# Gate and up products of a gated MLP by seven block products per 128 features, the down product as a stage of its own

## The chip, the cores and the metric

The kernel runs on one core of a Trainium2 chip. The engines have short names in the profile: PE is the matrix engine (PEld its weight loads), DVE the vector engine, ACT the scalar engine, POOL the GpSimd engine, and SP issues most of the DMAs. The metric is the device time of one execution in microseconds (us), as the median of the runs.

## The reference, cut to what matters

One encoder layer over 512 tokens of 2048 features, all in float32: a mixer (retention and state-space heads), a gated MLP with 5632 features, and a gated per-layer input. The change is in the MLP and in the output projection that feeds it:

```python
hn = rmsnorm(h, norm_mix_w[i])
...
h = h + jnp.concatenate([ret, ssd], axis=-1) @ w_out[i]
hn = rmsnorm(h, norm_ffn_w[i])
h = h + conv_glu_ffn(hn, ffn_w_gate[i], ffn_w_up[i], ffn_conv_w[i], ffn_conv_b[i], ffn_w_down[i])
...
def conv_glu_ffn(h, w_gate, w_up, conv_w, conv_b, w_down):
    gate = depthwise_conv(h @ w_gate, conv_w, conv_b)
    return (jax.nn.gelu(gate, approximate=True) * (h @ w_up)) @ w_down
```

The convolution runs over tokens, with three taps. The norm of a token is a factor that the kernel applies after the products.

## The kernel before, in words

Activations lie feature-major: 128 features on the partitions, 512 tokens in the row. Each large product is float32 split exactly into two float32r parts, hi and lo, and takes three passes (`mm3`: hi by hi, hi by lo, lo by hi). A chunk is 128 output features over K = 2048, so 16 times 3 matmuls of 512 columns; each matmul loads its own 128 x 128 weights.

Weights come as a stream of units of 128 x 1024 (512 KB). SP fetches a unit into one of four `raw` tiles (`fetch`), ACT copies it to `whi` (L195), DVE subtracts to get `wlo` (L196), and there are three `whi`/`wlo` pairs. `next_unit` calls `split` two units ahead, so the split of unit i+2 waits until PE has left unit i-1, and has the time of two units.

The stages in order: mixer, output projection (16 chunks, DVE adds the residual at L874, ACT and POOL add up squares for the norm), MLP, per-layer input. After the projection every chunk of h is scaled and split into `xh`, `xl` (`operands`, L241, L242); the token norm (`token_norm`) goes through PE, DVE, POOL and PE again and ends in `Rb`, the norm on every partition. In the MLP, `ffn_order` lists 44 chunks "f" (gate, then up, two units each) and 11 groups "d" of the down product, each group after the four chunks that feed it. `ffn_chunk` takes the products out of PSUM with DVE (L887, L897), convolves (ACT L888, DVE L889 and L891), applies the gelu on ACT (L893), multiplies (L898) and splits the result into `ah`, `al` (L901, L902), which stay on chip. `down_group` has 8 units of 24 matmuls and adds to `h_t` in place (L917, 16 times a group). h stays on chip from the projection to the end.

Each engine runs its own instructions in order and waits on semaphores. The order is what a scheduler made of the program's order and of `tc.high_priority()`; what it made is shown below.

Of the kernel before, what the change touches and what calls it, by code (L numbers as in the profile page):

```python
# [17 lines left out]
F32 = mybir.dt.float32  # L18
# [8 lines left out]
P = 128  # L27
T = 512
# [25 lines left out]

XBC_ORDER = [8, 12, 10, 0, 1, 2, 3, 9, 11, 4, 5, 6, 7]
# [23 lines left out]
def layer(ctx: ExitStack, tc: tile.TileContext, xT, pT, pos, w_xbc, w_v, w_z, w_q, w_k, w_g,  # L79
# [42 lines left out]
    # ---------------------------------------------------------------- weight stream  # L122
# [19 lines left out]
    for n in range(KC):  # L142
        add_chunk(w_out, n)
    NG = FC // 4

    def ffn_order():
        order = [("f", c) for c in range(4)]
        for g in range(NG):
            if g + 1 < NG:
                order.append(("f", 4 * g + 4))  # L150
            order.append(("d", g))
            if g + 1 < NG:
                order += [("f", 4 * g + i) for i in (5, 6, 7)]
        return order

    for kind, i in ffn_order():
        if kind == "f":
            add_chunk(w_gate, i)
            add_chunk(w_up, i)
        else:  # L160
            for u in range(8):
                units.append(w_down[i, u])
# [12 lines left out]

    def fetch(i, pieces=1):
        if i < len(units) and i not in raws:
# [3 lines left out]
            raws[i] = r  # L181

    def split(i, pool=None, pieces=1):
        if i < len(units) and i not in splits:
            with tc.high_priority():
                fetch(i)
                r = raws[i]
# [10 lines left out]
                del raws[i]  # L198
                if not pool:
                    for j in range(i + 1, i + FETCH + 1):  # L200
                        fetch(j)
# [30 lines left out]
    cosR = const.tile([P, T], F32, name="cosR")  # L232
    sinR = const.tile([P, T], F32, name="sinR")
# [3 lines left out]
    # operand tiles: hi / lo of the moving activations, one per 128 features  # L237
# [18 lines left out]
    def gemm_chunk(xops):  # L256
        """128 output features x 512 tokens over K = 2048"""
# [5 lines left out]
    def ssq_mm(bank, sq, first, last):  # L263
        """bank[:, blk] += sum over the 128 partitions of sq[:, token]"""
# [11 lines left out]
    def diag_tokens(r, pool):  # L276
        """[128 tok, nb] column form -> hi and lo of its diagonal blocks"""
# [3 lines left out]
        dh = pool.tile([P, NB, P], F32R, name="bc_dh")[:, 0:nb]  # L281
        dl = pool.tile([P, NB, P], F32R, name="bc_dl")[:, 0:nb]
# [7 lines left out]
    def bcast_mm(dh, dl):  # L290
        """the column form on every partition: PSUM [128, 128 nb]"""
# [6 lines left out]
    def silu_of_half(dst, uh, th):  # L298
        """dst = silu(2 * uh)"""
# [24 lines left out]
    def token_norm(ss, pool, then=None):  # L324
        """two stages: sums and their rstd; Rb, the norm of each token on every partition"""
        box = []

        def one():
# [3 lines left out]
            box.append(diag_tokens(rcol, pool))  # L332
# [8 lines left out]
    # ================================================================ mixers  # L341
# [14 lines left out]
    # ---- start: x in, operands, token norms  # L356
    with tc.tile_pool(name="start", bufs=1) as st:
# [52 lines left out]
    # ---- SSD  # L410
    mix = ExitStack()
# [8 lines left out]
    # dt = softplus(.) and the decays; v's tile lends the room  # L420
# [706 lines left out]
```

## Time and profile before

| | |
|---|---|
| device time, median of 3 runs | 2573.64 us (2573.16 to 2577.39) |
| span of the profiled execution, first to last instruction | 2570.3 us |
| so outside the span, against the median | 3.3 us |
| PE busy | 2515.8 us (98%) |
| DVE, ACT, POOL busy | 1263.8, 804.3, 196.2 us |
| DMA moved | 257.33 MB, mean 100 GB/s |

The profile is of one execution. A matmul's length in it holds the pipeline's fill and drain, so the distance between two starts tells more than the length: successive matmuls overlap. The same holds, by a little, for instructions on DVE and ACT. The granted clock of PE (PEclk) is 1.00 when it has its full 2.4 GHz and 0.50 at 1.2 GHz.

### The profile page before, as it was taken

What the parts mean: (1) busy time and instruction counts of PE and PEld (TensorE: products, weight loads), DVE (VectorE), ACT (ScalarE), POOL (GpSimd) and SP (SyncE); (2) the same over time, 40 slices, a digit from 0 to 9 for tenths busy, and PEclk for the clock granted to TensorE, in tenths of its full rate; (3) what the DMA queues carried; (4) which work ended last, traced back from release to release, by engine and by line L of the source; (5) the groups of instructions that cost most, each with busy time, mean ns of one, the idle gap of its engine ahead of it and who ended that gap; (6) DMA issues with size and microseconds to landing.
All of it is one profiled execution on the core that took longest, in us unless ns stands there. A gap on an engine that the chain in (4) does not pass through costs nothing. (4 is left out here: it accounts for less than half of the span.)

```text
span 2570.3 us, 27344 instructions
## 1 busy us (share of the span) xinstructions
PE 2515.8 (98%) x11160; PEld 2068.8 (80%) x11160; DVE 1263.8 (49%) x1510; ACT 804.3 (31%) x1034; POOL 196.2 (8%) x136
## 2 busy tenths in 40 slices
PE   8988999999999999999999999999999999999997
PEld 6866678888888888888888888888888888887886
DVE  7887552665552254444344444444434444447344
ACT  4332343444332242222222222222222222225342
POOL 6023210000001100000000000000000000003111
PEclk9989999999999999999999999999999999999998
DMA  5333323232233333333333333333323333332332
GB/s 191 108 91 108 97 95 93 88 96 88 82 123 123 117 96 99 96 94 98 98 98 99 94 95 98 99 99 96 94 98 99 98 98 94 96 98 91 98 96 85
DMA packets 91326, 257.33 MB, mean 100 GB/s; under 512 B 8736, under 2 KB 29472, under 8 KB 91200
## 3 DMA queue, kind: packets, MB, share of 16 engines
q1 hardware_dynamic: 91056, 255.58, 32.0%
q8 instruction: 87, 1.43, 0.2%
q14 instruction: 39, 0.32, 0.0%
q10 hardware_dynamic: 144, 0.01, 0.0%
HBM read 251.29 MB, written 4.26 MB: 99 GB/s over the span
## 5 line engine op out<-in xcount | busy, mean ns | idle before, releaser
L211 PE MATMUL mm<-xh,whi 128*128 128x512 f32 (+1 forms) x2528 | 988.1, 391 | 5.8 <-ACT whi L195 5.0
L213 PE MATMUL mm<-xh,wlo 128*128 128x512 f32 (+1 forms) x2528 | 983.5, 389 | 4.0 <-DVE wlo L196 4.0
L212 PE MATMUL mm<-xl,whi 128*128 128x512 f32 (+1 forms) x2528 | 984.0, 389 | 2.0 <-DVE xl L242 2.0
L195 ACT CAST whi<-raw 128x1024 fp32r<-128x1024 f32 (+1 forms) x439 | 460.8, 1050 | 1282.7 <-PE mm L212 1194.1
L196 DVE TENSOR_TENSOR wlo<-raw,whi 128x1024 fp32r<-128x1024 f32 (+1 forms) x439 | 547.6, 1248 | 545.1 <-ACT whi L195 545.0
L211 PEld LDWEIGHTS mm<-xh,whi 128*128 128x128 f32 x2528 | 476.4, 188 | 105.3 <-ACT whi L195 5.5
L212 PEld LDWEIGHTS mm<-xl,whi 128*128 128x128 f32 x2528 | 476.1, 188 | 104.5 <-DVE xl L242 5.6
L213 PEld LDWEIGHTS mm<-xh,wlo 128*128 128x128 f32 x2528 | 476.2, 188 | 103.5 <-DVE wlo L196 5.6
L211 PE MATMUL mm<-ah,whi 128*128 128x512 f32 x704 | 274.1, 389 | 0.5 <-DVE h L917 0.5
L213 PE MATMUL mm<-ah,wlo 128*128 128x512 f32 x704 | 273.9, 389 | 0.0
L212 PE MATMUL mm<-al,whi 128*128 128x512 f32 x704 | 273.9, 389 | 0.0
L917 DVE TENSOR_TENSOR h<-h,mm 128x512 f32<-128x512 f32 x176 | 120.8, 687 | 207.6 <-PE mm L213 207.6
L322 POOL TENSOR_TENSOR ssq<-ssq,sq 128x512 f32<-128x512 f32 x52 | 80.9, 1556 | 1794.2 <-issue 1414.5
L211 PEld LDWEIGHTS mm<-ah,whi 128*128 128x128 f32 x704 | 132.1, 188 | 28.7 <-DVE h L917 0.7
L213 PEld LDWEIGHTS mm<-ah,wlo 128*128 128x128 f32 x704 | 132.1, 188 | 27.5
L212 PEld LDWEIGHTS mm<-al,whi 128*128 128x128 f32 x704 | 132.1, 188 | 27.4
L639 PE MATMUL mm<-whi,xh 128*128 128x512 f32 x256 | 106.4, 416 | 14.1 <-ACT v L649 9.2
L897 DVE TENSOR_TENSOR fup<-mm,Rb 128x512 f32<-128x512 f32 x44 | 30.4, 692 | 146.3 <-PE mm L213 146.3
L887 DVE TENSOR_TENSOR fpre<-mm,Rb 128x512 f32<-128x512 f32 x44 | 30.4, 692 | 144.2 <-PE mm L213 144.2
L640 PE MATMUL mm<-wlo,xh 128*128 128x512 f32 x256 | 100.9, 394 | 0.2 <-DVE wlo L196 0.2
L641 PE MATMUL mm<-whi,xl 128*128 128x512 f32 x256 | 100.8, 394 | 0.0
L639 PEld LDWEIGHTS mm<-whi,xh 128*128 128x128 f32 x256 | 48.9, 191 | 28.1 <-ACT v L649 10.0
(228 smaller groups left out, 1462.3 us busy)
## 6 DMA issues: line engine op xcount, KB each, us to landing
raw<-in_w_gate SPq DMA_DIRECT2D x88, 512.0 KB, 3.6
raw<-in_w_up SPq DMA_DIRECT2D x88, 512.0 KB, 3.6
raw<-in_w_down SPq DMA_DIRECT2D x88, 512.0 KB, 3.5
raw<-in_w_out SPq DMA_DIRECT2D x32, 512.0 KB, 3.6
raw<-in_w_ple SPq DMA_DIRECT2D x32, 512.0 KB, 3.6
raw<-in_w_xbc SPq DMA_DIRECT2D x25, 512.0 KB, 3.7
bc<-rows_d SPq DMA_DIRECT2D x16, 512.0 KB, 5.9
raw<-in_w_v SPq DMA_DIRECT2D x16, 512.0 KB, 3.5
```

Source lines behind the costliest of these rows:

```text
L195: S.copy(hi[:, sl], r[:, sl])
L196: V.tensor_tensor(lo[:, sl], r[:, sl], hi[:, sl].bitcast(F32), op=ALU.subtract)
L211: TE.matmul(out, lh, rh, start=start, stop=False)
L212: TE.matmul(out, lh, rl, start=False, stop=False)
L213: TE.matmul(out, ll, rh, start=False, stop=stop)
L322: G.tensor_tensor(self.acc, self.acc, sq, op=ALU.add)
L639: TE.matmul(banks[b], xh[:, sl], wh, start=(k == 0), stop=False)
L640: TE.matmul(banks[b], xh[:, sl], wl, start=False, stop=False)
L641: TE.matmul(banks[b], xl[:, sl], wh, start=False, stop=(k == KC - 1))
L887: V.tensor_tensor(pre, gb, Rb, op=ALU.mult)
L897: V.tensor_tensor(up, ub, Rb, op=ALU.mult)
L917: V.tensor_tensor(h_t[n], h_t[n], bank, op=ALU.add)
```

## The change

For each chunk of 128 features the weights are taken as four blocks of 128 x 1024: gate and up, each for the first and the second half of K. The activations are taken as four blocks too: two halves of K, each for the first and the second 256 tokens. Gate and up for both halves of the tokens then are a 2 x 2 block product, and it is made from seven products instead of eight, each with K = 1024 and 256 columns (`prod`: 8 times 3 matmuls). Three of the seven weight forms are sums (`weight_form`: four adds of 128 x 1024 on DVE a chunk, three of them in place), and each form is split to hi and lo as a unit was. The seven activation forms (`singles`, `sums`) are made once, from h scaled by the norm's weights, for 8 pairs of chunks (chunk j and j + 8, so the projection's order is changed to give them in pairs); for three pairs (EARLY) during the projection, for five after it. All are kept as hi and lo in `E`.

h goes to DRAM (`h_d`) and the 44 results of `ffn_chunk` too (`acts_d`), by DMAs that POOL issues. The down product runs after all 44 chunks, in six groups of K (five of two weight rows, one of one); the activations of a group are read back through a `fup` tile by POOL's DMAs and split by ACT and DVE, those of the next group during the current one. The matmuls of the down product are as many and as large as before; it adds to h 6 times 16 times instead of 11 times 16.

```diff
+DOWN = [(0, 1), (2, 3), (4, 5), (6, 7), (8, 9), (10,)]
...
+    for c in range(FC):
+        for k in FORMS:
+            units.append((c, k))
+    for ds in DOWN:
+        for u in range(8):
+            for d in ds:
+                units.append(w_down[d, u])
...
+        if k == 2:
+            V.tensor_tensor(w11, w11, w12, op=ALU.add)
+            gu_sum[c] = f6 = gu_pool[1].tile([P, 1024], F32, name="wsum", bufs=1)
+            V.tensor_tensor(f6, w11, w22, op=ALU.add)
+            return f6
+        if k == 3:
+            return w11
+        if k == 4:
+            V.tensor_tensor(w12, w12, w22, op=ALU.add)
+            return w12
+        if k == 5:
+            return w22
+        V.tensor_tensor(w21, gu_sum.pop(c), w21, op=ALU.add)
+        return w21
...
+    SLOT = (0, 1, 4, 3, 5, 6, 2)
...
+    def form_split(j, a, n, src):
+        hi, lo = (e[:, a:a + n] for e in E[j])
+        S.copy(hi, src)
+        V.tensor_tensor(lo, src, hi.bitcast(F32), op=ALU.subtract)
...
+    def singles(j):
+        form_split(j, 0, 1, xw[j][:, 0:1])
+        form_split(j, 1, 2, xw[j][:, 2:4])
...
+        if which == 0:
+            t = late_p.tile([P, 2, HT], F32, name="es", bufs=2)
+            V.tensor_tensor(t[:, 0], x21, x22, op=ALU.subtract)
+            V.tensor_tensor(t[:, 1], t[:, 0], x11, op=ALU.subtract)
+            form_split(j, 3, 2, t)
+        else:
+            V.tensor_tensor(x21, x11, x21, op=ALU.subtract)
+            V.tensor_tensor(x12, x12, x22, op=ALU.subtract)
+            V.tensor_tensor(x12, x12, x21, op=ALU.subtract)
+            form_split(j, 5, 2, xw[j][:, 1:3])
...
+        ss.add(hc)
+        nc.gpsimd.dma_start(h_d[n], hc)
...
+    for j in range(EARLY, KP):
+        singles(j)
+    for j in range(EARLY, KP):
+        sums(j, 0)
+    for j in range(EARLY, KP):
+        sums(j, 1)
+    norm_stages = token_norm(ss, late_p, tag="es")
...
+        hi, lo = (w.rearrange("p (k n) -> p k n", n=P) for w in next_unit())
+        for j in range(KP):
+            eh, el = (e[:, slot] for e in E[j])
+            mm3(out, hi[:, j], lo[:, j], eh, el, start and j == 0, stop and j == KP - 1, True)
+        tick()
...
+        R, PQ = mm_bank(), mm_bank()
+        r, p, q = R[:, 0:HT], PQ[:, 0:HT], PQ[:, HT:T]
+        prod(r, SLOT[0], True, True)
+        if c == 0:
+            norm_stages[0]()
+        prod(p, SLOT[1], True, True)
+        if c == 0:
+            norm_stages[1]()
...
+            S.copy(ab[:, 0:HT], r)
+        prod(r, SLOT[2], False, True)
...
+            S.activation(ab[:, HT:T], r, AF.Copy, scale=-1.0)
+        prod(q, SLOT[3], True, True)
...
+            S.copy(cc, q)
+        prod(r, SLOT[4], False, True)
...
+            V.tensor_tensor(up[:, HT:T], cc, r, op=ALU.subtract)
+        prod(q, SLOT[5], False, True)
...
+            V.tensor_tensor(s[:, :, 0:HT], PQ.rearrange("p (n t) -> p n t", n=2),
+                            ab.rearrange("p (n t) -> p n t", n=2), op=ALU.add)
+        V.tensor_tensor(up, up, Rb, op=ALU.mult)
+        prod(r, SLOT[6], False, True)
...
+        V.tensor_tensor(acc, up, acc, op=ALU.mult)
+        nc.gpsimd.dma_start(acts_d[c], acc)
...
+        a = main.tile([P, T], F32, name="fup", bufs=3)
+        nc.gpsimd.dma_start(a, acts_d[c])
+        hi = pool.tile([P, T], F32R, name=f"ah{c % 8}")
+        lo = pool.tile([P, T], F32R, name=f"al{c % 8}")
+        S.copy(hi, a)
+        V.tensor_tensor(lo, a, hi.bitcast(F32), op=ALU.subtract)
...
+    for c in chunks(0):
+        load_act(c, sides[0].p)
+    for n in range(KC):
+        nc.gpsimd.dma_start(h_t[n], h_d[n])
```

Where the instructions stand. DVE in a chunk of the middle of the MLP, before (L196 is the split of a weight unit, L887 and L897 take the products out of PSUM):

```order
L887 TENSOR_TENSOR fpre_10369<-mm_10308,Rb_74 128x512
L196 TENSOR_TENSOR wlo_10378<-raw_10245,whi_10377 128x1024
L889 SCALAR_TENSOR_TENSOR facc_10370<-fpre_10369,vec_69,facc_10370 128x511
L891 SCALAR_TENSOR_TENSOR facc_10370<-fpre_10369,vec_69,facc_10370 128x511
L196 TENSOR_TENSOR wlo_10408<-raw_10275,whi_10407 128x1024
L897 TENSOR_TENSOR fup_10437<-mm_10376,Rb_74 128x512
L898 TENSOR_TENSOR fup_10437<-fup_10437,facc_10370 128x512
L196 TENSOR_TENSOR wlo_10445<-raw_10313,whi_10444 128x1024
L902 TENSOR_TENSOR al_10441<-fup_10437,ah_10440 128x512
```

The same in the changed kernel, from the subtraction that follows product 4 (counted from 0) to the split of form 3 of the next chunk (`wlo` from `rawB` or `wsum` is the split of a weight form, L217, L219, L224, L228 are the weight sums):

```order
L1037 TENSOR_TENSOR s_11290<-cc_11289,mm_11227 128x256
L247 TENSOR_TENSOR wlo_11384<-rawB_11127,whi_11383 128x1024
L217 TENSOR_TENSOR rawB_11127<-rawB_11127,rawB_11190 128x1024
L1040 TENSOR_TENSOR s_11290<-mm_11228,ab_11288 128x2x256
L224 TENSOR_TENSOR rawB_11190<-rawB_11190,rawB_11192 128x1024
L219 TENSOR_TENSOR wsum_11459<-rawB_11127,rawB_11192 128x1024
L247 TENSOR_TENSOR wlo_11416<-rawB_11158,whi_11415 128x1024
L1042 TENSOR_TENSOR s_11290<-s_11290,Rb_80 128x512
L228 TENSOR_TENSOR rawB_11158<-wsum_11459,rawB_11158 128x1024
L247 TENSOR_TENSOR wlo_11462<-wsum_11459,whi_11461 128x1024
L247 TENSOR_TENSOR wlo_11490<-rawB_11127,whi_11489 128x1024
L1047 TENSOR_TENSOR s_11290<-s_11290,Rb_80 128x512
```

Before, one or two weight splits stand between two instructions that read PSUM; now all four weight sums and the splits of forms 0 to 3 follow L1037, with one reader of PSUM among them (L1040).

DVE at the start of the MLP, before (`xl` is the lo part of the last activations, L273 to L287 make the token norm's diagonal blocks):

```order
L242 SCALAR_TENSOR_TENSOR xl13_6469<-h_5344,vec_69,xh13_6468 128x512
L242 SCALAR_TENSOR_TENSOR xl14_6473<-h_5344,vec_69,xh14_6472 128x512
L242 SCALAR_TENSOR_TENSOR xl15_6477<-h_5344,vec_69,xh15_6476 128x512
L196 TENSOR_TENSOR wlo_6512<-raw_6319,whi_6511 128x1024
L273 TENSOR_SCALAR rstd_t_6531<-mx_6526 128x4
L284 CAST bc_rh_6534<-rcol_77 128x4
L285 TENSOR_TENSOR bc_dh_6536<-cst_70,bc_rh_6534 128x512
L286 TENSOR_TENSOR bc_rl_6535<-rcol_77,bc_rh_6534 128x4
L287 TENSOR_TENSOR bc_dl_6537<-cst_70,bc_rl_6535 128x512
L196 TENSOR_TENSOR wlo_6570<-raw_6356,whi_6569 128x1024
```

In the changed kernel, the end of that work (L932 is the lo part of an activation form, L951 to L953 are the sums of the last two, L338 and L340 the same diagonal blocks; the waits are in brackets):

```order
L247 TENSOR_TENSOR wlo_6743<-raw_6333,whi_6742 128x1024 [waits PE_49,Activation_49]
L932 TENSOR_TENSOR El5_6537<-xw5_6177,Eh5_6536 128x512 [waits Activation_49]
L952 TENSOR_TENSOR xw6_6318<-xw6_6318 128x256
L951 TENSOR_TENSOR xw7_6459<-xw7_6459 128x256
L953 TENSOR_TENSOR xw6_6318<-xw6_6318 128x256 [waits DVE_49]
L952 TENSOR_TENSOR xw7_6459<-xw7_6459 128x256
L338 TENSOR_TENSOR es_6655<-cst_76,bc_rh_6653 128x512
L932 TENSOR_TENSOR El6_6539<-xw6_6318,Eh6_6538 128x512 [waits Activation_49]
L953 TENSOR_TENSOR xw7_6459<-xw7_6459 128x256 [waits DVE_49]
L340 TENSOR_TENSOR es_6656<-cst_76,bc_rl_6654 128x512
L932 TENSOR_TENSOR El7_6541<-xw7_6459,Eh7_6540 128x512 [waits Activation_49]
L247 TENSOR_TENSOR wlo_6773<-raw_6329,whi_6772 128x1024 [waits PE_49,Activation_49]
```

The diagonal blocks of the norm, which came right after the last activation, now come behind nearly all of the late activation forms.

POOL at the end of the MLP, before (L322 adds squares, L274 is the power of the norm; no DMA is on this queue):

```order
L322 TENSOR_TENSOR ssq_15254<-ssq_15254,sq_15480 128x512
L322 TENSOR_TENSOR ssq_15254<-ssq_15254,sq_15503 128x512
L322 TENSOR_TENSOR ssq_15254<-ssq_15254,sq_15520 128x512
L274 TENSOR_TENSOR rcol_77<-rstd_t_15692,mhalf_73 128x4
L322 TENSOR_TENSOR ssq_15727<-ssq_15727,sq_15796 128x512
```

In the changed kernel, from its first instruction for the down stage (L1070 reads an activation, L1091 a chunk of h, L1055 writes an activation):

```order
L1070 DMA fup_16730<-acts_d_5346 128x512 [waits DMASW3_49,PE_49,Activation_49]
L1070 DMA fup_16736<-acts_d_5346 128x512 [waits DMASW4_49]
L1070 DMA fup_16742<-acts_d_5346 128x512 [waits DMASW5_49]
L1091 DMA h_16726<-h_d_5345 128x512 [waits DMASW6_49]
L1091 DMA h_16726<-h_d_5345 128x512 [waits DMASW7_49]
L1091 DMA h_16726<-h_d_5345 128x512 [waits DMASW0_49]
L1070 DMA fup_16748<-acts_d_5346 128x512 [waits DMASW3_49,DMASW1_49,DVE_49]
L1070 DMA fup_16754<-acts_d_5346 128x512 [waits DMASW4_49,DMASW2_49,DVE_49]
L1091 DMA h_16726<-h_d_5345 128x512
L1070 DMA fup_16760<-acts_d_5346 128x512 [waits DMASW5_49,DVE_49]
L1055 DMA acts_d_5346<-acc_16711 128x512 [waits DVE_49]
L1091 DMA h_16726<-h_d_5345 128x512 [waits DMASW6_49]
```

POOL now issues the loads of the first activations one by one, with loads of h and a store between them, and those from the fourth on wait for DVE to free a `fup` tile.

## Rows read from the trace of the kernel before

**Rows 1.** The page's part 1: busy time, share of the span, instructions of each engine.

```profile
PE 2515.8 (98%) x11160; PEld 2068.8 (80%) x11160; DVE 1263.8 (49%) x1510; ACT 804.3 (31%) x1034; POOL 196.2 (8%) x136
```

**Rows 2.** Stretches, from the MLP's first matmul to the down product's last.

```profile
913.08:2350.40 1437.32, 1436.82 (x6341) 1189.18 (x6340) 638.78 (x725) 381.54 (x425) 20.02 (x13) 1.00 0.31 96
```

**Rows 3.** The timeline of PE in the last chunk, 256 columns: start, length (us).

```profile
2539.39 0.28 PE L211 MATMUL mm<-xh,whi 128*128 128x256 f32 x1
2539.50 0.28 PE L212 MATMUL mm<-xl,whi 128*128 128x256 f32 x1
...
2548.74 0.50 PE L267 MATMUL mx<-ones,ssq 128*128 128x1 f32 x4
```

**Rows 4.** The timeline of weight loads (PEld) in the same stretch.

```profile
2539.39 0.19 PEld L212 LDWEIGHTS mm<-xl,whi 128*128 128x128 f32 x1
2539.50 0.19 PEld L213 LDWEIGHTS mm<-xh,wlo 128*128 128x128 f32 x1
```

**Rows 5.** Groups by form: count | busy us, mean ns of one | idle before.

```profile
L196 DVE TENSOR_TENSOR wlo<-raw,whi 128x1024 fp32r<-128x1024 f32 x437 | 546.2, 1251 | 544.2 <-ACT whi L195 544.1
L195 ACT CAST whi<-raw 128x1024 fp32r<-128x1024 f32 x437 | 459.5, 1052 | 1281.6 <-PE mm L212 1194.1 <-PE mm L641 55.4 <-issue 26.7
...
L322 POOL TENSOR_TENSOR ssq<-ssq,sq 128x512 f32<-128x512 f32 x52 | 80.9, 1556 | 1794.2 <-issue 1414.5 <-ACT sq L320 379.2
L888 ACT ACTIVATE facc<-fpre,vec 128x512 f32<-128x512 f32 x44 | 35.6, 810 | 1.4 <-DVE fpre L887 1.4
...
L891 DVE SCALAR_TENSOR_TENSOR facc<-fpre,vec,facc 128x511 f32<-128x511 f32 x44 | 33.0, 751 | 1.5
L887 DVE TENSOR_TENSOR fpre<-mm,Rb 128x512 f32<-128x512 f32 x44 | 30.4, 692 | 144.2 <-PE mm L213 144.2
...
L569 DVE TENSOR_TENSOR bc<-bc,A 128x1024 f32<-128x1024 f32 x8 | 12.3, 1535 | 17.7 <-POOL bc L566 17.7
...
L1023 DVE TENSOR_TENSOR h<-h,mx 128x256 f32<-128x256 f32 x12 | 4.4, 413 | 0.4 <-ACT facc L1014 0.4
L274 POOL TENSOR_TENSOR rcol<-rstd_t,mhalf 128x4 f32<-128x4 f32 x3 | 3.1, 1020 | 16.6 <-DVE rstd_t L273 16.6
```

**Rows 6.** The timeline of DVE in MLP chunks: start, length (us), idle before.

```profile
1207.17 0.69 DVE L887 TENSOR_TENSOR fpre<-mm,Rb 128x512 f32<-128x512 f32 x1 [3.35 <-PE mm L213]
1208.03 1.23 DVE L196 TENSOR_TENSOR wlo<-raw,whi 128x1024 fp32r<-128x1024 f32 x1 [0.17 <-ACT whi L195]
...
1218.05 0.69 DVE L897 TENSOR_TENSOR fup<-mm,Rb 128x512 f32<-128x512 f32 x1 [3.35 <-PE mm L213]
1218.77 0.69 DVE L898 TENSOR_TENSOR fup<-fup,facc 128x512 f32<-128x512 f32 x1
1219.38 1.22 DVE L196 TENSOR_TENSOR wlo<-raw,whi 128x1024 fp32r<-128x1024 f32 x1
1220.52 0.68 DVE L902 TENSOR_TENSOR al<-fup,ah 128x512 fp32r<-128x512 f32 x1
```

**Rows 7.** The timeline of ACT in the same chunk.

```profile
1206.94 1.05 ACT L195 CAST whi<-raw 128x1024 fp32r<-128x1024 f32 x1 [4.38 <-PE mm L212]
```

**Rows 8.** The timeline of PE there, the last two matmuls of a weight unit.

```profile
1206.51 0.39 PE L212 MATMUL mm<-xl,whi 128*128 128x512 f32 x1
1206.74 0.39 PE L213 MATMUL mm<-xh,wlo 128*128 128x512 f32 x1
```

**Rows 9.** Stretches of 2 us around PE's longest wait.

```profile
252.00:254.00 2.00, 0.00 (x0) 0.00 (x0) 0.04 (x1) 0.00 (x0) 0.00 (x0) 1.00 0.80 228
256.00:258.00 2.00, 0.01 (x1) 0.01 (x1) 0.10 (x1) 1.33 (x4) 1.87 (x2) 0.50 0.61 218
262.00:264.00 2.00, 0.80 (x4) 0.37 (x3) 1.81 (x2) 2.00 (x4) 0.00 (x0) 1.00 0.00 0
```

**Rows 10.** DMA issues by line: count, KB each, us to landing.

```profile
raw<-in_w_gate SPq DMA_DIRECT2D x88, 512.0 KB, 3.6
...
bc<-rows_d SPq DMA_DIRECT2D x16, 512.0 KB, 5.9
...
fup<-in_xT SPq DMA_DIRECT2D x16, 256.0 KB, 2.6
```

More of the change, by code (lines that the diff above doesn't have):

```diff
@@ L53 @@
 N_VEC = _n
+FORMS = range(7)
+KP = KC // 2
+EARLY = 3
+DOWN = [(0, 1), (2, 3), (4, 5), (6, 7), (8, 9), (10,)]
 XBC_ORDER = [8, 12, 10, 0, 1, 2, 3, 9, 11, 4, 5, 6, 7]
@@ L141, in layer @@
         add_chunk(w_g, h)
-    for n in range(KC):
+    OUT_ORDER = [n for j in range(KP) for n in (j, j + KP)]
+    for n in OUT_ORDER:
         add_chunk(w_out, n)
[L144 to L162, printed above, removed]
+    for c in range(FC):
[5 more added lines that the diff above has]
+                units.append(w_down[d, u])
     for n in range(KC):
@@ L197, in split @@
                 splits[i] = (hi, lo)
-                del raws[i]
                 if not pool:
-                    for j in range(i + 1, i + FETCH + 1):
+                    ahead = FETCH
+                    if i + FETCH < len(units) and isinstance(units[i + FETCH], tuple):
+                        ahead = 2 * FETCH
+                    for j in range(i + 1, i + ahead + 1):
                         fetch(j)
@@ new lines, in layer, with prod @@
+    ox.close()
+    opx.close()
+    g1 = ExitStack()
+    fb_p = g1.enter_context(tc.tile_pool(name="fb", bufs=1, reuse_waits="tile"))
+    gu_pool[1] = fb_p
+    for j in range(EARLY, KP):
+        form_tiles(j, fb_p)
+    for j in range(EARLY, KP):
+        singles(j)
+    for j in range(EARLY, KP):
+        sums(j, 0)
+    for j in range(EARLY, KP):
+        sums(j, 1)
+    norm_stages = token_norm(ss, late_p, tag="es")
+    m1 = None
+    def prod(out, slot, start, stop):
+        hi, lo = (w.rearrange("p (k n) -> p k n", n=P) for w in next_unit())
[3 more added lines that the diff above has]
+        tick()
@@ L865, in layer @@
+    for c in range(FC):
+        ffn_chunk(c)
+    g1.close()
+    fa.close()
     main = ctx.enter_context(tc.tile_pool(name="main", bufs=1, reuse_waits="tile"))
@@ new lines, in layer, with open_group, chunks, down_group @@
+    sides = {}
+    def open_group(g):
+        sides[g] = e = ExitStack()
+        e.p = e.enter_context(tc.tile_pool(name=f"acts{g}", bufs=1, side="left" if g % 2 else "right",
+                                           reuse_waits="tile"))
+    def chunks(g):
+        return [4 * d + k for d in DOWN[g] for k in range(4)]
+    open_group(0)
+    for c in chunks(0):
+        load_act(c, sides[0].p)
+    for n in range(KC):
+        nc.gpsimd.dma_start(h_t[n], h_d[n])
+    def down_group(g, ss):
+        last = g + 1 == len(DOWN)
+        if not last:
+            open_group(g + 1)
+            ahead = chunks(g + 1)
+        for u in range(8):
+            banks = [mm_bank(), mm_bank()]
+            for i, d in enumerate(DOWN[g]):
+                hi, lo = (w.rearrange("p (k n) -> p k n", n=2 * P) for w in next_unit())
+                for nn, bank in enumerate(banks):
+                    sl = slice(nn * P, (nn + 1) * P)
+                    for k in range(4):
+                        ah, al = acts[4 * d + k]
+                        mm3(bank, hi[:, k, sl], lo[:, k, sl], ah, al, i == 0 and k == 0,
+                            i + 1 == len(DOWN[g]) and k == 3)
+            for nn, bank in enumerate(banks):
+                n = 2 * u + nn
+                with tc.high_priority():
+                    V.tensor_tensor(h_t[n], h_t[n], bank, op=ALU.add)
+                if ss:
+                    ss.add(h_t[n])
+            if not last and u < len(ahead):
+                load_act(ahead[u], sides[g + 1].p)
+            tick()
+        if last:
+            sides[g].close()
+        else:
+            sides[g].close()
```

205 lines of the change are left out of this document (115 added, 90 removed).

## The prediction

> **What bounds the kernel now.** I read the page's busy times first. PE is busy 98% of a span of 2570.3 us, DVE 49%, ACT 31% [rows 1]: PE is the bound if it is dense and not merely overlapped with waits. So the stretch that the change rebuilds comes next, from the MLP's first matmul to the last of the down product: 1437.32 us, of which PE is busy 1436.82, at a granted clock of 1.00, DVE 639, ACT 382 [rows 2]. Its work is 44 x 2 x 48 = 4224 matmuls for gate and up and 11 x 8 x 24 = 2112 for down, 6336 of 512 columns: 1437.3 / 6336 = 0.2268 us each (a dozen small matmuls of the norm are in it). PE starts a matmul every 0.227 us there and waits for nobody; only fewer or shorter matmuls, or new waits, can change it.
>
> The new matmuls have 256 columns, each with its own weight load. The last chunk of the kernel is computed in two halves of the tokens, so the trace holds that form: 78 starts from 2539.39 to 2548.74 [rows 3], 0.1199 us each. That is 53% of 0.2268, not 50%; seven products instead of eight therefore give 7/8 x 2 x 0.53 = 0.925 of the time, not 0.875.
>
> **Gate and up.** Removed: 4224 x 0.2268 = 958.0 us. Added: 44 x 7 x 24 = 7392 matmuls x 0.1199 = 886.3 us. That is -71.7 us if PE stays dense. A product takes 24 x 0.1199 = 2.88 us, a chunk 20.1 us.
>
> Does DVE keep up? It is in order, and the spacing of its instructions counts, not their length: a split of 1024 follows its predecessor's start by 0.61 and is followed after 1.14 us (1218.77, 1219.38, 1220.52); an instruction that needs its predecessor's result waits for its end and 0.04 more (1218.05 to 1218.77) [rows 6]. The weight sums have no row; two-input instructions of 1024 lie between 1.25 us (the split, 437 of them) and 1.54 us (L569) [rows 5]. I take the split, which has the same size and two SBUF inputs as they have. A chunk is then 11 x 1.14 (7 splits, 4 sums) + 4 x 0.61 + 2 x 0.75 + 0.41 = 16.9 us of 20.1 [rows 5, 6]. ACT has 7 x 1.05 and six smaller ones of at most 0.81, below 12.3 us [rows 5].
>
> The tight place is the chain shown by the order, from the end of product 4 to the split of form 2 of the next chunk. PE's release reaches ACT 0.04 us after the last read of `whi` ends, and DVE 0.04 after ACT ends (1206.51 + 0.39 to 1206.94; 1207.99 to 1208.03) [rows 6 to 8]; a 256-column matmul is 0.28 long, so ACT begins 0.08 after product 5 has begun. Then 1.05 + 0.04 for `whi`, split 1.29, sum 1.14, PSUM 0.61, sums 2 x 1.14, split 1.14, `up` 0.61, sum 1.14, split 1.29: 10.7 us in all. PE needs that `wlo` at the third matmul of product 2: 4 x 2.88 + 0.24 = 11.8 us later. The slack is 1.1 us, so I cost the steady chunk at nothing. The waits on PSUM have more: each accumulator is read while a 2.88 us product runs on the other bank. Behind a late DVE the splits of all later forms queue, and PE waits for them.
>
> The weights are as many bytes, 2 MB per 20.1 us, fetched 8 forms ahead (23 us) against 3.6 us to landing [rows 10]: hidden.
>
> **Start of the MLP.** Before, this is seamless. Now no activation form of five pairs exists when the projection ends, and DVE makes them. Counting from the last projection matmul: DVE adds the residual until 0.9, ACT squares until 1.6, POOL issues a store of h and adds (1.56 us) until about 3.5, PE sums, DVE reads at 4.1, POOL's power takes 1.02 [rows 5], and DVE, which is in order, goes on at 5.4. From there to the second diagonal block and the splits around it stand 7 x 1.14 (2 sums, 5 splits) + 17 x 0.61 (15 lo parts, 2 diagonals) + 24 x 0.34 (256 wide: 0.41 long, less the 0.07 that a successor overlaps) = 26.5 us, with 2 us of in-place waits and one wait for PE: 34 us. Products 0 and 1, which follow the lo parts pair by pair, end near 14.5, product 3 near 25. The norm's broadcast is next on PE and waits for a diagonal block near 31.7. ACT then copies `Rb` and the first product (1.0), and four products remain: 31.7 + 0.5 + 1.0 + 11.5 = 44.7. PE's clock: after 8 us without matmuls the granted clock stood at 0.50 and was 1.00 again six us later [rows 9]; PE idles 7 us here, which I put at +2. So the first chunk takes 47 us instead of 20: +27. Bounds: 16 if POOL and DVE overlap better and the clock holds; 40 if every DVE instruction takes its full length (34 becomes 39) and all five last products run at half speed.
>
> **Down.** The matmuls are the same: 2112 x 0.2268 = 479.0. The first activations must come back from DRAM after the last MLP matmul, since their tiles lie where the activation forms were. POOL-issued DMAs have no row; 256 KB from SP lands in 2.6 us, the slowest kind of row takes 5.9 [rows 10]. I take 3 with a microsecond of POOL per issue (its shortest instruction in rows 5 is 1.02): first at 3.4, `ah0` and `al0` at 4.8, the fourth activation at 11, the eighth at 18, because three `fup` tiles cycle and loads of h stand in POOL's queue between them. PE does what it can meanwhile (11 of 21.8 us of the first two weight rows): +8. Bounds: 4, with issue at nothing and 2.6; 18, with 5.9 in each of three rounds. DVE's 80 fewer adds of h (11 x 16 to 6 x 16) were hidden and gain nothing. Later groups load during the group before: 8 loads in 87 us. The hand-over to the per-layer input keeps its form: 0, give or take 2; likewise the projection, where DVE gains 4.5 us of work per pair in a 21.8 us window.
>
> [...]
>
> **Sum.** 886.3 + 27 + 479.0 + 8 = 1400.3 against 1437.3: -37 us. The span becomes 2533.3; the median of the runs lies 3.3 us above the span of the profiled execution, so 2536.6.
>
> **Rivals.**
> 1. DVE becomes the bound. If its 1024-wide instructions, with sums in place, take the 1.54 us of L569, the seven in the chain cost 7 x 0.4 = 2.8 us more, less 1.1 of slack: 1.7 x 44 = +75, so 2611, slower. It decides against the change from 1.1 + 37/44 = 1.94 us, that is from 1.42 us per instruction. For it: DVE's work in a chunk nearly doubles and has only 3 us to spare. Against: 437 splits average 1.25.
> 2. The hand-overs eat the gain: 72 us instead of 35, with both upper bounds and 14 more in the first chunks of each stage. 2574, no change.
> 3. Weight loads become the bound. PEld is 80% busy already [rows 1] and a load lasts 0.19 us [rows 4]; one after the other, 7392 x 0.19 would be 1404 instead of 886: about 3055, slower. The Trainium skill, "Perfetto Trace Analysis", section "Identifying the Most-Contended Engine", judges PE by just this share and not by matmul time, which would make the change a loss. Against: at 256 columns loads start 0.11 to 0.12 us apart and overlap [rows 4], 78 times in a row [rows 3].
> 4. The hand-overs cost half, since the scheduler's order lets PE go on earlier: 35 becomes 18, so 2519.
>
> **How the numbers follow.** My forecast has 0.77, its own range 2521 to 2558 (both lower bounds; 40 for the start, 18 for down). Rival 1 has 0.08, rival 2 0.06, rival 3 0.02, rival 4 0.07. For 8 in 10 I take 2516 to 2564. The runs can tell a change of 0.2% (5 us): faster is the forecast, rival 4 and a part of rival 2, 0.87; same 0.04; slower 0.09.
>
> **What would show it.** Matmul starts 0.12 us apart through the MLP, PE over 99% busy in a middle chunk of 20.1 us, and 43 of them. If chunks take longer and PE waits for `wlo`, rival 1 is at work, and the lengths of the sums say why; if it waits with weight loads back to back, rival 3. In the first chunk PE should wait for the lo parts and then long for the diagonal blocks, some 27 us in all; at the start of down for `ah` and `al`, some 8. The prediction is wrong if the 256-column pitch does not hold at full rate for 886 us, or if either hand-over costs more than twice its term.

## The result, and the profile after

The changed kernel takes 2544.27 us (median of 4 runs, 2541.68 to 2545.18) against 2573.4 of the kernel before on the same chip: a ratio of 0.9887, 95% interval 0.9873 to 0.9901, so 29 us faster. Forecast were 2536.6, between 2516 and 2564. The profiled execution has a span of 2541.9 us, 28.4 less than before. By the terms of the sum:

| term | predicted, us | profile, us |
|---|---|---|
| gate and up, 44 steady chunks | 886.3 | 883.0 (44 x 20.067) |
| first chunk, over a steady one | +27 | +27.5 (47.52 - 20.07) |
| hand-over to down | +8 | +7.2 (5.2 to the first matmul, 2.0 in the first group) |
| the matmuls of down | 479.0 | 486.6 |
| per-layer input | 0 | +4.1 |
| ahead of the MLP | 0 | +0.6 |
| all, against before | -37 | -28.4 |

The terms that were hard to size came out right by size. The two that were carried over unchanged (down and the per-layer input) are the ones that failed. Part 1 of the page, the answer to [rows 1]:

```profile
PE 2464.6 (97%) x14328; PEld 2165.9 (85%) x14328; DVE 1628.3 (64%) x1882; ACT 1005.2 (40%) x1374; POOL 257.4 (10%) x256
```

The stretches that answer to [rows 2] (length, then busy time and count of PE, PEld, DVE, ACT, POOL, then the granted clock, DMA share, GB/s): the first chunk, a middle chunk, the wait for down, its first three groups, and the rest to the end.

```profile
913.64:961.16 47.52, 32.52 (x179) 28.45 (x178) 31.43 (x57) 19.60 (x33) 2.88 (x3) 0.68 0.28 95
1402.82:1422.89 20.07, 20.07 (x171) 20.07 (x169) 17.19 (x19) 9.78 (x13) 0.54 (x1) 1.00 0.36 120
1824.27:1829.27 5.00, 0.11 (x1) 0.00 (x1) 1.85 (x3) 1.99 (x4) 3.19 (x6) 1.00 0.78 272
1829.27:1920.89 91.62, 91.62 (x385) 73.01 (x386) 42.54 (x51) 27.04 (x35) 16.35 (x30) 0.98 0.57 192
1920.89:2007.97 87.08, 87.08 (x386) 72.07 (x384) 35.60 (x40) 21.53 (x25) 4.39 (x8) 1.00 0.39 121
2007.97:2097.58 89.61, 89.61 (x385) 72.08 (x384) 35.61 (x40) 21.50 (x25) 4.39 (x8) 1.00 0.38 118
2317.86:2541.90 224.04, 206.96 (x943) 168.49 (x941) 94.31 (x121) 83.38 (x113) 31.18 (x25) 0.97 0.28 93
```

The same last stretch of the kernel before, from its last down matmul:

```profile
2350.40:2570.30 219.90, 202.76 (x943) 168.89 (x941) 94.66 (x121) 83.19 (x113) 31.17 (x25) 0.97 0.30 95
```

Read the second and the third group of down side by side: 384 matmuls each (the counts take in one or two at the edges), the clock at 1.00, PE busy all the time, and yet 87.08 against 89.61 us. The last stretch shows the same: as many matmuls as before, the same clock, 4.2 us more PE time. No wait explains it; the matmuls themselves are further apart. The timeline of PE (start, length) in the first and in the second group:

```profile
1899.89 0.39 PE L264 MATMUL mm<-ah,whi 128*128 128x512 f32 x1
1900.12 0.40 PE L265 MATMUL mm<-al,whi 128*128 128x512 f32 x1
1900.36 0.39 PE L266 MATMUL mm<-ah,wlo 128*128 128x512 f32 x1
1900.59 0.39 PE L264 MATMUL mm<-ah,whi 128*128 128x512 f32 x1
...
1959.69 0.39 PE L264 MATMUL mm<-ah,whi 128*128 128x512 f32 x1
1959.91 0.39 PE L265 MATMUL mm<-al,whi 128*128 128x512 f32 x1
1960.14 0.39 PE L266 MATMUL mm<-ah,wlo 128*128 128x512 f32 x1
1960.37 0.39 PE L264 MATMUL mm<-ah,whi 128*128 128x512 f32 x1
```

Three matmuls take 0.70 us in the first group and 0.68 in the second, 0.2333 against 0.2267 each. The groups alternate between the two ends of SBUF (`open_group`: "right" for even groups). The trace holds no addresses; the built program does. The right end is at byte 229344 of a partition, 96 past a multiple of 128, so `ah0` of an even group starts at 196576, 96 past one, and `ah0` of an odd group at 140160, a multiple of 128. `xh`, `xl` of the per-layer input lie at the right end too (163808), and so do the three early pairs of activation forms (186336). In the kernel before, the moving operands of down and of the per-layer input (the activations, as against the loaded weights) lie on multiples of 128. That became the first theory to test.

### The profile page after: what moved, and what is told of

Read it like the earlier page. It is cut to its first block, busy times and chain, and to the rows that moved or that the text cites. A ratio compares the mean times of both kernels' runs of the same rounds, so it can differ in the third digit from the quotient of the medians.

```text
span 2541.9 us, 35008 instructions
## 1 busy us (share of the span) xinstructions
PE 2464.6 (97%) x14328; PEld 2165.9 (85%) x14328; DVE 1628.3 (64%) x1882; ACT 1005.2 (40%) x1374; POOL 257.4 (10%) x256
## 5 line engine op out<-in xcount | busy, mean ns | idle before, releaser
L265 PE MATMUL mm<-El,whi 128*128 128x256 f32 x2464 | 700.9, 284 | 4.9 <-DVE El L932 4.9
L266 PE MATMUL mm<-Eh,wlo 128*128 128x256 f32 x2464 | 698.0, 283 | 0.8 <-DVE wlo L247 0.8
L264 PE MATMUL mm<-Eh,whi 128*128 128x256 f32 x2464 | 695.7, 282 | 3.0 <-ACT Eh L931 1.3
L265 PEld LDWEIGHTS mm<-El,whi 128*128 128x128 f32 x2464 | 471.5, 191 | 6.4 <-DVE El L932 6.3
L264 PEld LDWEIGHTS mm<-Eh,whi 128*128 128x128 f32 x2464 | 472.2, 192 | 4.5 <-ACT Eh L931 1.8
L266 PEld LDWEIGHTS mm<-Eh,wlo 128*128 128x128 f32 x2464 | 470.8, 191 | 1.1 <-DVE wlo L247 1.0
L264 PE MATMUL mm<-xh,whi 128*128 128x512 f32 (+1 forms) x1120 | 440.8, 394 | 6.3 <-ACT whi L246 5.1
L266 PE MATMUL mm<-xh,wlo 128*128 128x512 f32 (+1 forms) x1120 | 437.1, 390 | 3.2 <-DVE wlo L247 3.1
L265 PE MATMUL mm<-xl,whi 128*128 128x512 f32 (+1 forms) x1120 | 436.7, 390 | 2.0 <-DVE xl L295 2.0
L266 PEld LDWEIGHTS mm<-xh,wlo 128*128 128x128 f32 x1120 | 211.4, 189 | 49.0 <-DVE wlo L247 4.5
L266 PEld LDWEIGHTS mm<-ah,wlo 128*128 128x128 f32 x704 | 132.4, 188 | 29.3
```

Source lines behind the costliest of these rows:

```text
L264: TE.matmul(out, lh, rh, start=start, stop=False, skip_group_check=skip)
L265: TE.matmul(out, lh, rl, start=False, stop=False, skip_group_check=skip)
L266: TE.matmul(out, ll, rh, start=False, stop=stop, skip_group_check=skip)
```

## The experiments

Two theories on the 11.7 us that were not forecast (7.6 in down, 4.1 in the per-layer input). A: a matmul is slower when its moving operand starts off a boundary. B: the end of the memory, or the transfers running beside it, make it slower. On the first chunk and the hand-over: the order of single instructions decides (C), or the sum of DVE's work and the loads' landing do (D). Times are medians; ratios are to the kernel before in the same job.

**A tile of 32 bytes at the right end.**

```diff
+    pad_p = ctx.enter_context(tc.tile_pool(name="pad", bufs=1, side="right"))
+    pad_t = pad_p.tile([P, 8], F32, name="pad")
+    V.memset(pad_t, 0.0)
     fa_p = fa.enter_context(tc.tile_pool(name="fa", bufs=1, side="right", reuse_waits="tile"))
```

> The changed kernel with a 32-byte tile at the right end of SBUF, so that every tile allocated from that end starts at a multiple of 64 bytes instead of 32 past one. Nothing else moves. Theory A (a 512-column matmul streams slower from an address 32 past a multiple of 64): the down groups 0, 2 and 4, whose activations lie at that end, go from about 0.2333 to 0.2268 us per matmul (1152 x 0.0065 = -7.5 us), the per-layer input goes from 224.0 back to about 219.9 us (-4.1); the 256-column products, at 2.867 us with three of eight pairs off the boundary, stay or go to 24 x 0.120 = 2.88 (0 to +4 us). Sum: -8 to -12 us, so 2532 to 2536. Theory B (the slower groups come from POOL's transfers or from which end of the memory is read): no change, 2544.

2533.33 us, ratio 0.9845 (0.9831 to 0.986). Groups 1 and 2 of down, and the per-layer input:

```profile
1917.88:2004.94 87.06, 87.06 (x385) 72.11 (x384) 35.53 (x40) 21.52 (x25) 4.37 (x8) 1.00 0.38 121
2004.94:2092.85 87.91, 87.91 (x385) 72.20 (x384) 35.63 (x40) 21.52 (x25) 4.37 (x8) 1.00 0.38 120
2311.42:2532.70 221.28, 204.17 (x943) 168.92 (x941) 94.34 (x121) 83.25 (x113) 31.22 (x25) 0.97 0.28 94
```

A move of 32 bytes takes most of the excess away, at the same end and with the same transfers beside it: B falls. It is not all of it. These tiles now start 64 past a multiple of 128, and group 2 still takes 0.85 us more than group 1, 0.2289 us a matmul.

**The kernel before, pushed off the boundary.**

```diff
+    pad_p = ctx.enter_context(tc.tile_pool(name="pad", bufs=1))
+    pad_t = pad_p.tile([P, 8], F32, name="pad")
     op = ctx.enter_context(tc.tile_pool(name="op", bufs=1))
```

> The kernel before with a 32-byte tile ahead of the activation operands, so that all moving operands start 32 bytes past a multiple of 64; weights and the order of the instructions stay. Theory A (address): 6336 matmuls of gate, up and down at 0.2327 to 0.2333 instead of 0.2268, the MLP stretch 1474 to 1478 us instead of 1437, and with the other large products (about 3300 more) the whole kernel +55 to +62 us, 2628 to 2636. Theory B: no change, 2573.

2634.77 us, ratio 1.0242 (1.0227 to 1.0257): 63 us slower than the kernel before in the same job (2571.83), from 32 bytes. PE in a chunk of its MLP:

```profile
1149.70 0.39 PE L214 MATMUL mm<-xl,whi 128*128 128x512 f32 x1
1149.94 0.40 PE L215 MATMUL mm<-xh,wlo 128*128 128x512 f32 x1
1150.17 0.39 PE L213 MATMUL mm<-xh,whi 128*128 128x512 f32 x1
1150.40 0.40 PE L214 MATMUL mm<-xl,whi 128*128 128x512 f32 x1
```

0.2333 us a matmul, and the weights of these products have not moved: theory A, at the upper end of what it allowed.

**The 256-column form by itself, without the seven products.**

```diff
-        gb = gemm_chunk(xops)
+        gb = gemm_halves(xops)      # each unit: 24 matmuls on columns 0:256, then 24 on 256:512
...                                  # and the same for the up product
```

> The kernel before, with each gate and up matmul of 512 columns done as two of 256 (8448 instead of 4224, the weights loaded for each), everything else as it was. It tests the price of the 256-column form without the seven products. Theory of the prediction (0.1195 to 0.12 us each in the long run): gate and up 1009 to 1014 instead of 958 us, so 2625 to 2629. If the form cost exactly half of a 512-column matmul: 2573. If it held only beside the changed kernel's other work, or weight loads were the bound (0.19 each): 2573 + 8448 x 0.19 - 958 = above 3200.

2629.39 us, ratio 1.0222 (1.0205 to 1.0239), +57.6 for 52 to 56 expected. The two halves are accumulated in turn in one PSUM bank, which changes the sums of gate and up; the instructions and their sizes are as described. A stretch of it holds 169 matmuls in 20 us:

```profile
1000.00:1020.00 20.00, 20.00 (x169) 20.00 (x168) 8.49 (x10) 4.80 (x6) 0.00 (x0) 1.00 0.31 89
```

The 57.6 us more make 8448 matmuls of 0.1202 us, so the form costs 0.12 in this kernel too, 53% of a whole matmul. Of the change, then, halving the columns costs 56 us (8448 x 0.12 = 1014 for 958), and seven products instead of eight bring 1014 down to 887.

**One and two more weight sums a chunk.**

```diff
             V.tensor_tensor(f6, w11, w22, op=ALU.add)
+            V.tensor_tensor(f6, w11, w22, op=ALU.add)   # in the second run, twice
```

> The changed kernel with one of the four weight sums of a chunk done twice, the same values again: 1.14 us more on DVE in the chain from product 4 to the split of form 2. Theory of the chain (in the trace that split ends 1.2 us before PE needs it): PE still waits for nothing in a steady chunk, 0 to +4 us, 2544 to 2548. Rival (DVE has reserve of 3 us a chunk, only its sum counts): the same, so this run alone doesn't part them. Rival 1 of the prediction (DVE already at the edge): +1.1 x 43 = +49.

> The same with that sum done three times: 2.28 us more in the chain, DVE's sum 19.4 of 20.07 us. Theory of the chain: 2.28 less 1.2 of slack, 1.1 us of waiting for wlo in each of 43 chunks, +47 us, 2591. Rival (only the sum of DVE's work counts): 0, 2544.

One more: 2550.18 us, ratio 0.9911 (0.9895 to 0.9928); a chunk takes 20.18 instead of 20.07, so 1.14 us is just past the slack. Two more: 2616.87 us, ratio 1.0169 (1.0154 to 1.0184), 26 us above the expectation, a chunk 21.68, +1.61. DVE in the changed kernel, from product 4's subtraction to the split of form 2, and the matmul that needs it (the third of product 2):

```profile
1417.42 0.42 DVE L1037 TENSOR_TENSOR s<-cc,mm 128x256 f32<-128x256 f32 x1 [0.75 <-PE mm L266]
...
1426.46 1.22 DVE L247 TENSOR_TENSOR wlo<-wsum,whi 128x1024 fp32r<-128x1024 f32 x1
...
1428.86 0.28 PE L266 MATMUL mm<-Eh,wlo 128*128 128x256 f32 x1
```

The same with two more sums:

```profile
1410.81 0.42 DVE L1039 TENSOR_TENSOR s<-cc,mm 128x256 f32<-128x256 f32 x1 [0.75 <-PE mm L268]
...
1420.98 0.68 DVE L1049 TENSOR_TENSOR s<-s,Rb 128x512 f32<-128x512 f32 x1
...
1422.72 1.22 DVE L249 TENSOR_TENSOR wlo<-wsum,whi 128x1024 fp32r<-128x1024 f32 x1
...
1423.20 0.39 PE L266 MATMUL mm<-Eh,whi 128*128 128x256 f32 x1 [0.44 <-ACT whi L248]
...
1423.99 0.39 PE L268 MATMUL mm<-Eh,wlo 128*128 128x256 f32 x1 [0.29 <-DVE wlo L249]
```

From L1037 to the split it was 9.04 us and is 11.91 with two more: 2.28 for the sums and 0.6 because the scheduler now has L1049 ahead of the split. That 0.6, in each of 43 chunks, matches the 26 us above the expectation. PE pays 1.61 of the 2.87, all of it between the end of product 1 and the first matmuls of product 2. The bracket shows only the wait that ends last: the scheduler has also drawn two matmuls of product 3 ahead of the one that needs `wlo` (the line at 1423.20 is the first of them), and PE waits for their `whi` on the way. They give it 0.24 us more of slack than in the changed kernel, 1.26 in all. DVE's sum would have had room; the chain decides, as forecast.

**The late forms behind the norm.**

```diff
-    for j in range(EARLY, KP):
-        sums(j, 1)
     norm_stages = token_norm(ss, late_p, tag="es")
...
             norm_stages[1]()
+            for j in range(EARLY, KP):
+                sums(j, 1)
             late.close()
```

> The changed kernel with one loop moved: the last two activation forms of the five late pairs are made after the token norm's diagonal blocks instead of before them. Theory (in the first chunk PE waits for DVE's order: the diagonal blocks stand behind five times 1.6 us of late forms): products 2 to 6 start about 8 us earlier, the first chunk takes about 40 us instead of 47.5, so 2536. Rival (DVE's sum of work bounds the chunk, in whatever order): PE then waits for the same lo parts in products 4 and 5, 0 to -3 us, 2541 to 2544.

2542.39 us, ratio 0.9881 (0.9866 to 0.9896), not told apart from the changed kernel. The first chunk takes 45.5 us. PE waited 4.77 us for the diagonal block and then 0.95 for `ab` in the changed kernel:

```profile
943.78 0.80 PE L347 MATMUL mx<-es,ones_r 128*128 128x512 f32 x1 [4.77 <-DVE es L338]
...
947.07 0.58 PE L264 MATMUL mm<-Eh,whi 128*128 128x256 f32 x1 [0.95 <-ACT ab L1028]
```

With the loop moved the first wait is 0.43 us, and the other has grown (PE's list of waits: us in total, times, longest):

```profile
PE mm L264 <- ACT ab L1028: 6.9, 1, 6.9
```

ACT, in order, shows why: the copy of the first product out of PSUM, which product 2 waits for, stands behind the casts of the moved forms, and each of these waits for DVE.

```profile
943.39 0.62 ACT L931 CAST Eh<-xw 128x512 fp32r<-128x512 f32 x1 [1.71 <-DVE xw L953]
945.34 0.62 ACT L931 CAST Eh<-xw 128x512 fp32r<-128x512 f32 x1 [1.33 <-DVE xw L953]
946.13 0.62 ACT L931 CAST Eh<-xw 128x512 fp32r<-128x512 f32 x1 [0.17 <-DVE xw L953]
946.65 0.36 ACT L1028 COPY ab<-mm 128x256 f32<-128x256 f32 x1
```

By the number the rival (DVE's sum) seemed right; by the profile one order had only taken the place of another.

**The late forms behind that copy too, four early pairs.**

```diff
-EARLY = 3
+EARLY = 4
...
             S.copy(ab[:, 0:HT], r)
+        if c == 0:
+            for j in range(EARLY, KP):
+                sums(j, 1)
+            late.close()
```

`xw` of the early pairs has one buffer instead of two, for space. 

> The changed kernel with the last forms of the late pairs behind the norm's diagonal blocks and behind ACT's first copy out of PSUM, and with four pairs in place of three made during the projection. Theory (what PE waits for in the first chunk is the place of single instructions in DVE's and ACT's order; in the run that moved the loop alone the wait for the diagonal block went from 4.8 to 0.4 us and 6.9 us of waiting for that copy came in its place): both waits go, and one late pair less saves 3.9 us of DVE; the first chunk takes 34 to 38 us instead of 47.5, so 2530 to 2535. Rival (DVE's sum bounds it): only the pair's 3.9 us, 2540.

2541.81 us, ratio 0.988 (0.9866 to 0.9895), a miss by the time. The first two chunks:

```profile
914.14:943.41 29.27, 25.14 (x179) 22.15 (x177) 26.44 (x47) 15.69 (x26) 3.10 (x3) 1.00 0.42 134
943.41:969.21 25.80, 22.74 (x170) 21.92 (x169) 20.34 (x21) 12.12 (x15) 0.60 (x1) 0.93 0.32 114
```

The first chunk fell from 47.5 to 29.3: 10.9 us less idle, and 7.4 us less PE time for the same products, at a granted clock of 1.00 where it had been 0.68 in the mean. The pair that was made early stands for only 3.9 of these 18.2 us. But 5.5 us came back in the second chunk, where ACT waited for the weights to land,

```profile
942.31 1.05 ACT L246 CAST whi<-rawB 128x1024 fp32r<-128x1024 f32 x1 [3.68 <-DMA rawB<-in_w_gate]
```

and 6.5 at the hand-over (a wait of 11.4 us for 4.9), where POOL's queue had the last activation's store ahead of the loads, and that store waited for DVE:

```profile
1821.11 0.54 POOL L1057 DMA_DIRECT2D acts_d<-acc  x1 [14.77 <-DVE acc L1056]
1821.64 1.63 POOL L1072 DMA_DIRECT2D fup<-acts_d  x3
```

And PE, its first matmul of down:

```profile
1825.48 0.80 PE L264 MATMUL mm<-ah,whi 128*128 128x512 f32 x1 [11.35 <-ACT ah L1075]
```

C holds for the first chunk; the gain went into two new waits.

**The first three activations loaded early.**

```diff
+        if c == FC - 2:
+            ahead_p = g1.enter_context(tc.tile_pool(name="ahead", bufs=1, reuse_waits="tile"))
+            for k in range(3):
+                a = ahead_p.tile([P, T], F32, name="fup0", bufs=3)
+                nc.gpsimd.dma_start(a, acts_d[k])
...
+    with tc.high_priority():
+        for c, a in enumerate(first):
+            cast_act(c, a, sides[0].p)
```

> The changed kernel with the first three activations of the down product loaded into a tile of their own before the last two chunks of the MLP, so that their casts wait for PE alone. Theory (PE's 4.9 us at the start of down are the loads' issue and landing): the first down matmul starts about 2 us after the last of the MLP instead of 5.1; the fourth activation still comes about 4.5 us after the MLP's end and PE waits a little for it; -2 to -4 us, 2540 to 2542. Rival (the casts on ACT and DVE, queued behind the last chunk's work, bound it): 0 to -1.

2538.24 us, ratio 0.9866 (0.9851 to 0.9881). Down follows the MLP without a gap, more than expected:

```profile
1823.08 0.28 PE L266 MATMUL mm<-Eh,wlo 128*128 128x256 f32 x1
1823.20 0.63 PE L264 MATMUL mm<-ah,whi 128*128 128x512 f32 x2
```

The first group takes 92.6 instead of 91.6 us, since the fourth activation is as late as it was. The edit also puts the first three casts ahead by priority, so by itself it does not part the loads from the casts. The trace of the changed kernel does: there ACT stood idle for the first load to land.

```profile
1828.60 0.62 ACT L1073 CAST ah<-fup 128x512 fp32r<-128x512 f32 x1 [2.98 <-DMA fup<-acts_d]
```

So the 5.2 us were the loads, as forecast.

**Multiples of 128 everywhere, with the early loads.** The 32-byte tile is made 96 bytes (`[P, 24]`). 

> The changed kernel with both mends that gained by themselves: a 96-byte tile at the right end, so that all moving operands start at a multiple of 128 bytes (with 32 bytes they started 64 past one, and groups 2 and 4 of down took 87.9 us against 87.1 of the odd groups), and the early loads of the first three activations. If the price of the address goes by steps of 128 bytes, groups 2 and 4 take 87.1 us and the per-layer input 219.9; with -5 of the hand-over the sum is -12 to -16 us, 2528 to 2532. If 64 was already as good as 128 and the odd groups are faster for another reason: groups 2 and 4 stay at 87.9, 2532 to 2534.

2531.44 us, ratio 0.9838 (0.9824 to 0.9851). A middle chunk, groups 1 and 2, the per-layer input:

```profile
1420.00:1440.16 20.16, 20.16 (x170) 20.16 (x170) 17.18 (x19) 9.77 (x13) 0.54 (x1) 1.00 0.37 115
1920.61:2007.65 87.04, 87.04 (x385) 72.12 (x384) 35.63 (x40) 21.47 (x25) 4.37 (x8) 1.00 0.38 121
2007.65:2094.69 87.04, 87.04 (x385) 72.12 (x384) 35.65 (x40) 21.46 (x25) 4.37 (x8) 1.00 0.39 121
2312.29:2531.80 219.51, 202.35 (x943) 168.61 (x941) 94.32 (x121) 83.17 (x113) 31.15 (x25) 0.97 0.29 95
```

All groups are now alike and the per-layer input is where it was before the change: for 512 columns a multiple of 128 is enough and 64 is not. But a chunk of 256-column products went from 20.067 to 20.160 us, exactly 168 x 0.12: there the three pairs off the boundary had been a gain (20.067 both at 96 past it and, in the run with the 32-byte tile, at 64).

**All of it, with the two give-backs mended.** Two of the odd chunks' four weight tiles lie where nothing has to be waited for, and the last store goes by SP's queue:

```diff
-        nc.gpsimd.dma_start(acts_d[c], acc)
+        (nc.sync if c == FC - 1 else nc.gpsimd).dma_start(acts_d[c], acc)
```

> The same with the reordered first chunk and four early pairs, two of the four weight tiles of the odd chunks placed where nothing has to be waited for, and the last activation's store on SP's queue, so that it no longer stands ahead of POOL's loads. The reordered chunk took 29.3 us instead of 47.5 before, of which 5.5 came back in the second chunk (weights late) and 6.5 at the hand-over (POOL's queue). If these two were the cause of the give-back: first two chunks 50 to 53 us together instead of 68, no wait at the hand-over, 2512 to 2520. If DVE's backlog is what comes back in the second chunk: 55 us together, 2518 to 2524.

2511.02 us, ratio 0.9764 (0.9751 to 0.9778). The first two chunks:

```profile
910.41:939.67 29.26, 25.11 (x180) 22.17 (x179) 28.16 (x48) 16.64 (x27) 3.10 (x3) 1.00 0.47 154
939.67:960.53 20.86, 20.57 (x171) 20.27 (x170) 18.52 (x20) 10.96 (x14) 1.15 (x2) 1.00 0.38 126
```

50.1 us together, and the first matmul of down 0.12 us after the last of the MLP:

```profile
1807.12 0.28 PE L266 MATMUL mm<-Eh,wlo 128*128 128x256 f32 x1
1807.24 0.63 PE L264 MATMUL mm<-ah,whi 128*128 128x512 f32 x2
```

So what came back in the second chunk was the late weights and not DVE's backlog. At the hand-over this run does not part the moved store from the early loads, which alone had closed the gap of the changed kernel; that the store stood in the way is what POOL's queue showed above.

**The forms of the MLP alone off the boundary.** The changed kernel with the 96-byte tile, and all eight pairs of forms 32 past a multiple of 128. 

> The changed kernel with the 96-byte tile at the right end, and with all eight pairs of activation forms moved 32 bytes past a multiple of 128, so that only the 256-column products of the MLP read from off the boundary. With three of eight pairs off it a chunk took 20.067 us, with none 20.160. Theory (a 256-column matmul does not pay for the offset, and even gains by it): about 20.160 - 8/3 x 0.093 = 19.91 us a chunk, 44 x -0.16 = -7 us against the changed kernel, with -12 for down and the per-layer input, 2525 to 2528. Rival (a moving operand off the boundary costs in either form, and the mixture hid it): chunks above 20.16 us, 2534 or more.

2519.9 us, ratio 0.9796 (0.9782 to 0.9809). A middle chunk, and group 1:

```profile
1420.00:1439.69 19.69, 19.69 (x171) 19.69 (x170) 17.17 (x19) 9.85 (x14) 0.54 (x1) 1.00 0.40 122
1901.93:1988.97 87.04, 87.04 (x385) 72.07 (x384) 35.61 (x40) 21.54 (x25) 4.38 (x8) 1.00 0.38 121
```

0.1172 us a matmul instead of 0.1200: the direction of the theory, and twice its size, so the time is below what was expected.

**Both.** The kernel with everything mended, with the forms off the boundary. 

> The kernel with the reordered first chunk, early loads and all operands on multiples of 128 bytes, now with the activation forms of the MLP alone moved off them (96 past one for the four early pairs, 32 past one for the four late), the rest as it was. Theory (the two effects of the address are independent of the rest): 44 chunks x (20.160 - 19.693) = -20.5 us against 2511, so 2488 to 2494. If 96 past a multiple is not as good as 32 for the 256-column products, half of it: 2500.

2499.05 us, ratio 0.9718 (0.9705 to 0.9732), the fastest of all and 73 us below the kernel before. It is 5 us above the range of the theory and near the other case of the expectation (2500): a chunk takes 19.83, not 19.69. The four pairs that lie 96 past a multiple take 0.1196 us a matmul in the mean, the four at 32 past one 0.1165.

## Why the prediction was right, and where it was not

**Gate and up: right.** 78 starts in the last chunk gave 0.1199; the long run gives 0.1194 here and 0.1200 with all operands on the boundary. Rival 3 (weight loads) fell: PEld is busy for the whole of a middle chunk, and the matmuls still start 0.12 apart. In the experiment with all forms moved off the boundary PEld is just as full and a chunk is 0.4 us shorter, so a full PEld is not the floor here. The Trainium skill, "Perfetto Trace Analysis", section "Identifying the Most-Contended Engine", judges TensorE by the busy share of its weight loads, beside the share of peak arithmetic, and not by matmul time. Read by the weight loads alone, the MLP would have had no room at 20.07 us; the chunk of 19.69 us with the same share decides against that reading.

**The steady chunk at nothing: right, and near the edge.** The slack was put at 1.1 us. One more sum (1.14) makes PE late by 0.12, at the third matmul of product 2, so it was 1.0. Rival 1 needed sums that follow one another after 1.42 us or more; they follow after 1.14 and are 1.22 long (L219, L224, L228), like the split that stood in for them. Its price of 75 us set a length (1.54) against a distance (1.14); length against length (1.54 and 1.25) gives 41.

**Start of the MLP: right by size, its inner parts partly by luck.** The broadcast starts 30.1 us after the MLP's first matmul (31.7 forecast, from the last matmul of the projection), and four products remain, in 14.1 us (11.5 + 2). But the forecast put 25 of its 27 us on waits and 2 on the clock. PE idles only 15.0 us in that chunk (47.52 less 32.52) and works 12.4 us longer than in a steady one, at a granted clock of 0.68; that the two errors nearly cancel is luck. The clock was taken into account only in the last four products, which are 2.6 us late without a wait. By the reordered run it cost 7.4 us of PE time in the whole chunk; that the waits hid the rest is argued, not shown. And what was taken for DVE's work was DVE's and ACT's order: with one late pair less the same work leaves a chunk of 29.3 us.

**Hand-over: right by size.** 7.2 for 8. The first matmul comes after 5.2 us (4.8 forecast): the loads land after 4.1 us (median) at 0.55 of POOL each, for 3 and 1 in the sum, and these errors cancel. The other 2.0 us are not the later loads, which the forecast put at about 3: PE waits for none of them. They come with the clock, which the forecast left out here. After 4.9 us without matmuls the first 3.75 us of down ran at a granted clock of 0.54:

```profile
1829.27:1833.02 3.75, 3.75 (x10) 2.94 (x10) 3.36 (x5) 2.52 (x5) 1.64 (x3) 0.54 1.04 399
```

**Down and the per-layer input: wrong.** The step that failed is "The matmuls are the same: 2112 x 0.2268 = 479.0", and the same for the per-layer input at 0. Shape and number are the same; the address is not, since the change moved these tiles to the other end of SBUF. Three of six groups pay 2.53 us each and the per-layer input 4.1, together 11.7. The experiments show the cause from both sides, taking it away in two steps and giving it to the kernel before. These 11.7 us less the 3.3 gained in gate and up make 8.4; forecast and result lie 7.7 apart.

**Rivals 2 and 4** (the hand-overs eat all, or cost half) fell: the two came to 34.7 us for 35. A slip without weight: with its own bounds (40 and 18) the upper end of the forecast's own range is 2560 and not 2558.

## What to carry to other kernels

Where a change moves the operands of untouched matmuls, look up their addresses: "as many and as large as before" was worth 12 us here. A reorder pays only if the next in-order instruction on the same path is moved with it, so look at the wait that is second before trying the first. And between two stages an in-order queue should hold no store that waits for the old stage ahead of loads for the new.

## What the runs showed of the hardware

The start of the moving operand within 128 bytes sets the pace of float32r matmuls of 512 columns at full clock: on the boundary 0.2267 us, 64 past it 0.2289, 32 or 96 past it 0.2333. With 256 columns it goes the other way: on the boundary 0.1200, 32 past it 0.1172 where all pairs lie there. That holds for a chunk as a whole and not pair by pair: in the changed kernel the three pairs 96 past it start 0.1194, 0.1208 and 0.1192 us apart in the mean of 41 chunks, the next pair, on the boundary, 0.1161, and the last four 0.1200. Why the sign turns, and why 96 past it is worth less than 32 for 256 columns, stays open; no run varies the weights' address in these products. The first chunk's slow clock (0.68 granted in the mean) came with PE's waits and was gone, at 1.00, when 10.9 us of them were; after the 4.9 us at the hand-over it stood at 0.54 for 3.75 us, and with no gap there it was 1.00.
